# Attention keys stored by residue modulo 4, with the value rows and masks in that order

## The chip, the cores and the metric

The kernel runs on one core of one Trainium2 chip. The metric is device time in microseconds (us) of one execution. The core has five engines with queues of their own: TensorE (PE in the profile; its weight loads are listed as PEld), VectorE (DVE), ScalarE (ACT), GpSimd (POOL) and SyncE (SP), which here issues nearly all DMAs. Matrix products land in PSUM, eight banks of 2 KB per partition.

## The reference

One layer of a bidirectional encoder over 1024 positions of width 2048. A normalised input is multiplied by a large matrix; the columns feed 16 attention heads (64 wide), an HGRN2 recurrence, and gates; an output matrix, a residual, and a gated embedding follow. What matters here is the attention:

```python
DILATION_CFG = ((128, 1), (512, 4), (2048, 16))   # window, dilation

q = rope_partial(heads(aq, ATT_HEADS), pos) * (ATT_HD ** -0.5)
k = rope_partial(heads(ak, ATT_HEADS), pos)
v = heads(av, ATT_HEADS)
res = [dilated_band_attention(q, k, v, w, d) for (w, d) in DILATION_CFG]
outs = jnp.stack([r[0] for r in res])
lses = jnp.stack([r[1] for r in res])
alpha = jax.nn.softmax(lses, axis=0)
o_att = jnp.einsum('gbsh,gbshe->bshe', alpha, outs).reshape(B, S, ATT_W)
y_att = o_att * jax.nn.silu(ag.astype(f32))
```

A query attends to the positions at most 64 away (dilation 1), to those at most 256 away of the same residue modulo 4, and to those of the same residue modulo 16. The three are joined by their log denominators, which is one softmax over all of them, a key counting as often as it occurs.

## The kernel before

**Products in three parts.** Every large product is made of float32 data split in a high part (fp32r) and a low part (bf16): high times high, high times the weight's low part, low times the weight in bf16. A group of 128 output columns (`group_parts`, L95 to L110) takes four weight pieces of 512 rows. `piece` (L70 to L86) loads a piece on SP (`raw`), and makes `wh` on ScalarE (L83), `wl` on GpSimd (L84) and `wb` on VectorE (L85), each from a ring of three buffers. A piece is 24 matmuls of 512 columns, 12 for each half of the 1024 positions, and `group_parts` hands control back twice per piece, so that a group has eight parts. The sums stand in two of four PSUM banks called `gb`; the other four (`wk`) serve scores, transposes and outputs.

**Order.** A planner orders the instructions of each engine when the program is built, by their place in the program and by modelled durations, and each engine then runs its queue strictly in that order. Instructions marked with `high_priority` (the pieces) are drawn forward. Work that stands later in the program can be placed earlier where the planner thinks that an engine would wait.

**The attention stage** works on eight pairs of heads (`Pair`), two heads of 64 in 128 partitions.

- `keys` (L550 to L574) makes a group of 128 columns. For each half, `rope_evac` copies it to `araw` (ScalarE, L521), sends four small DMAs on SP to `apart` (L525, L526), multiplies on GpSimd (L528) and VectorE (L529), and the callback adds the two (L560). The sum is then split in three bf16 tiles `ak`: for each head a cast on ScalarE (L566), a DMA that puts a copy into the other 64 partitions (L568, L570), a subtraction on VectorE (L567), and at last a cast on VectorE (L572). Keys lie in order of position, 1024 a row.
- `queries` and `q_half` (L576 to L606) do the like for the queries, which are written by residue modulo 4 within each block of 128; the split is `aqt`.
- `scores` (L620 to L672) makes eight units per half: four dilated ones, one per residue, in which 128 queries meet 256 keys of that residue (`KS[s][:, h, i::4]`), and four local ones, in which 128 queries (reordered in `aql`, L633) meet 256 neighbouring keys from `wstart(i)`. A unit is six matmuls (L642): two heads, three products. VectorE adds the mask and takes the maximum (L647), ScalarE makes the exponential and its sum (L649). After every second unit one part of another group, the `fill`, is issued, so that TensorE has work. Small steps on VectorE (L657 to L670) then join the denominators.
- `values` (L674 to L718) scales the weights (L690, L692), transposes them on TensorE (L694), copies them out of PSUM (L697), and multiplies with the value rows: L710 dilated with `avc`, L707 local with `avn`.
- `loads` (L608 to L618) fetches `avc` by two DMAs and `avn` by three: eleven tiles of 128 positions, which the local windows share.
- `gate` (L720 to L731) is a group whose callback multiplies the output `ayt` (sigmoid on ScalarE, L727; VectorE, L728; GpSimd, L729).

The main loop (L806 to L827) sets how these follow: for pair n, `a.scores(0)` with parts of a's gate as fill, four parts of pair n+1's queries, `a.values(0)`, `a.scores(1)` with the other four as fill, then this:

```python
            run(bq)
            if b:
                if n:
                    run(g, 2)
                run(b.keys(), 9)
                b.q_half(0)
            a.values(1)
            run(g)
```

For pair 0 four gate parts come before its scores, so none are left at this point. Small tiles (`araw`, `apr`, `aq`, `sg`) share a ring of five (`h2`).

Of the kernel before, what the change touches and what calls it, by code (L numbers as in the profile page):

```python
# [12 lines left out]
F32 = mybir.dt.float32  # L13
# [4 lines left out]
ALU = mybir.AluOpType  # L18
# [27 lines left out]
class Kern:  # L46
# [367 lines left out]
    def att_consts(self, positions):  # L414
# [35 lines left out]
        V.tensor_scalar(d, d, NEG, -NEG, op0=ALU.mult, op1=ALU.add)  # L450
        V.scalar_tensor_tensor(m, m, -math.log(2.0), d, op0=ALU.mult, op1=ALU.add)
        e2 = self.h2("ae2").bitcast(I32)[:, :384]
        nc.gpsimd.iota(e2, pattern=[[1, 384]], base=-128, channel_multiplier=0)
        m = MK[:, 384:]
        V.tensor_scalar(m, e2, tf, None, op0=ALU.subtract)
        V.tensor_tensor(m, m, m, op=ALU.mult)
# [76 lines left out]
        self.tc.add_manual_dep(inst.ins, mark.ins.name, mybir.DependencyInfo(mybir.DependencyClass.NoSync, mybir.DependencyReason.DATA),  # L533
                               reason="issue order")

    starts = [0, 128] + [128 * j - 64 for j in range(1, 8)] + [768, 896]

    @staticmethod
    def wstart(i):
        return 0 if i == 0 else (768 if i == 7 else 128 * i - 64)  # L540
# [1 line left out]
    class Pair:  # L542
# [7 lines left out]
        def keys(self):  # L550
            K, nat = self.K, self.nat
            nc = K.nc
            V = nc.vector
            self.KS = [K.big.tile([128, 2, S], BF16, name=f"ak{i}", tag=t, bufs=n)
                       for i, (t, n) in enumerate((("X", 2), ("X", 2), ("O", 1)))]

            def sink(hf, p):
                def fin(a, b):
                    sl = slice(512 * hf, 512 * hf + 512)
                    V.tensor_tensor(a, a, b, op=ALU.add)  # L560
                    for s in range(3):
                        for h in range(2):
                            n, m = nat[h], nat[1 - h]
                            kd = self.KS[s][n, h, sl]
                            if s < 2:
                                nc.scalar.copy(kd, a[n])  # L566
                                V.tensor_tensor(a[n], a[n], kd, op=ALU.subtract)  # L567
                                nc.sync.dma_start(self.KS[s][m, h, sl], kd)  # L568
                                if s == 0:
                                    nc.sync.dma_start(self.KS[2][m, h, sl], kd)  # L570
                            else:
                                V.tensor_copy(kd, a[n])  # L572
                K.rope_evac(False, hf, p, fin)
            return K.group_parts(self.w_in, 1024 + 128 * self.hp, sink)  # L574

# [32 lines left out]
        def loads(self):  # L608
            K, vsrc = self.K, self.vsrc
            nc = K.nc  # L610
            self.vn = K.big.tile([128, 11, 128], F32, name="avn", tag="ht", bufs=1)
            self.vc = K.big.tile([128, 4, 2, 128], F32, name="avc", tag="hvt", bufs=1)
            for k in range(2):
                nc.sync.dma_start(self.vc[:, :, k], vsrc[512 * k:512 * k + 512, :].rearrange("(p r) e -> p r e", r=4))
            for i0, n in ((0, 2), (2, 7), (9, 2)):
                t0 = K.starts[i0]
                nc.sync.dma_start(self.vn[:, i0:i0 + n], vsrc[t0:t0 + 128 * n, :].rearrange("(c p) e -> p c e", p=128))
            self.yt = K.big.tile([128, S], F32, name="ayt", tag="gt", bufs=1)  # L618

        def scores(self, hf, fill):  # L620
            K, KS, QT = self.K, self.KS, self.QT
            nc = K.nc
            V = nc.vector
            sm = [K.big.tile([128, 2, 4, 256], F32, name=f"asm{h}", tag=("F2", "Q2")[h], bufs=1) for h in range(2)]
            own = K.sp.tile([128, 2, 2, 2, 4], F32, name="aown", bufs=1)
            oth = K.sp.tile([128, 2, 2, 2, 4], F32, name="aoth", bufs=1)
            for u, (loc, i) in enumerate(((0, 0), (0, 1), (1, 0), (0, 2), (1, 1), (0, 3), (1, 2), (1, 3))):
                w0 = K.wstart(4 * hf + i)
                sc = K.wk("asc")
                if loc:  # L630
                    ql = K.big.tile([128, 4, 4, 32], BF16, name="aql", tag="aql", bufs=3)
                    src = QT.rearrange("p h s (r i b) -> p (h s) r i b", i=4, r=4)[:, :, :, i]
                    (nc.gpsimd.tensor_copy if i % 2 else nc.scalar.copy)(ql, src)  # L633
                for h in range(2):
                    for s, sq in ((0, 0), (1, 0), (2, 1)):
                        if loc:
                            st = ql[:, 2 * h + sq].rearrange("p r b -> p (r b)")
                            mv = KS[s][:, h, w0:w0 + 256]
                        else:
                            st = QT[:, h, sq, 128 * i:128 * i + 128]  # L640
                            mv = KS[s][:, h, i::4]
                        nc.tensor.matmul(sc[:, 256 * h:256 * h + 256], st, mv, start=(h == 0 and s == 0),  # L642
                                         stop=(s == 2), skip_group_check=True)
                ms = 384 + (w0 - 128 * (4 * hf + i) + 128) if loc else 128 - 128 * hf
                for h in range(2):
                    d = sm[h][:, loc, i]
                    V.tensor_tensor_reduce(out=d, in0=sc[:, 256 * h:256 * h + 256], in1=K.MK[:, ms:ms + 256], scale=1.0,  # L647
                                           scalar=3.0e38, op0=ALU.add, op1=ALU.min, accum_out=own[:, 0, loc, h, i:i + 1])
                    nc.scalar.activation(d, d, AF.Exp, scale=-1.0, bias=own[:, 0, loc, h, i:i + 1],  # L649
                                         accum_out=own[:, 1, loc, h, i:i + 1])  # L650
                if u % 2:
                    next(fill, None)
            for x in range(4):
                for y in range(4):
                    o = oth[32 * x:32 * x + 32].rearrange("p s l h i -> p (s l h) i")[:, :, y]
                    w = own[32 * y:32 * y + 32].rearrange("p s l h i -> p (s l h) i")[:, :, x]
                    V.tensor_copy(o, w)  # L657
            m = K.sp.tile([128, 2, 2, 4], F32, name="afm", bufs=1)
            e = K.sp.tile([128, 2, 2, 2, 4], F32, name="afe", bufs=1)
            for l in range(2):  # L660
                V.tensor_tensor(m[:, l], own[:, 0, l], oth[:, 0, 1 - l], op=ALU.min)
                V.tensor_tensor(e[:, 1, l], m[:, l], oth[:, 0, 1 - l], op=ALU.subtract)
            V.tensor_tensor(e[:, 0], m, own[:, 0], op=ALU.subtract)
            nc.scalar.activation(e, e, AF.Exp)
            V.tensor_tensor(own[:, 1], own[:, 1], e[:, 0], op=ALU.mult)
            for l in range(2):
                V.tensor_tensor(e[:, 1, l], e[:, 1, l], oth[:, 1, 1 - l], op=ALU.mult)
            V.tensor_tensor(m, own[:, 1], e[:, 1], op=ALU.add)
            V.reciprocal(m, m)
            V.tensor_tensor(m, m, e[:, 0], op=ALU.mult)  # L670
            self.sm[hf] = sm
            self.fac[hf] = m  # L672

        def values(self, hf):  # L674
# [24 lines left out]
            def use(n):  # L699
                l, i = steps[n]  # L700
                P = pt[n // 2][:, n % 2]
                for c in range(2):
                    for h in range(2):
                        hs = slice(64 * h, 64 * h + 64)
                        if l:
                            t = K.starts.index(K.wstart(4 * hf + i) + 128 * c)
                            nc.tensor.matmul(o[hs, 128 * i:128 * i + 128], vn[:, t, hs], P[:, h, c],  # L707
                                             start=False, stop=(n == 7 and c == 1), skip_group_check=True)
                        else:
                            nc.tensor.matmul(ov[hs, :, i, :], vc[:, i, c, hs], P[:, h, c].rearrange("p (i b) -> p i b", i=4),  # L710
                                             start=(n == 0 and c == 0), stop=False, skip_group_check=True)
# [23 lines left out]
def tile_hybrid(ctx, tc, x, p, positions, w_in, w_out, g_pre, g_post, g_hg, lb_fwd, lb_bwd, w_pg, w_pp, g_ple, out):  # L735
# [54 lines left out]
    with tc.tile_pool(name="big", bufs=1) as big:  # L790
# [8 lines left out]
        def run(parts, n=8):  # L799
            for _ in range(n):  # L800
                next(parts, None)
# [5 lines left out]
        for n, a in enumerate(heads):  # L807
            b = heads[n + 1] if n < 7 else None
            a.loads()
            g = a.gate()  # L810
            if n == 0:
                run(g, 4)
            a.scores(0, g)
            bq = b.queries() if b else iter(())
            run(bq, 4)
            if n == 7:
                run(g, 2)
            a.q_half(1)
            a.values(0)
            a.scores(1, bq if b else islice(g, 2))  # L820
            run(bq)
            if b:
                if n:
                    run(g, 2)
                run(b.keys(), 9)
                b.q_half(0)
            a.values(1)  # L827
            run(g)
# [258 lines left out]
```

## Time and profile before

| | |
|---|---|
| Median of 3 runs | 2933.66 us (2931.59 to 2936.01) |
| Profiled execution | 2931.53 us, of which the profile's span is 2929.7 us |
| Granted TensorE clock | 0.99 of full speed |
| TensorE busy | 2793.9 us (95%) |
| VectorE, ScalarE, GpSimd busy | 1541.4, 1022.2, 1045.4 us |
| Attention stage | about 1260 to 2125 us of the span |
| DMA queues | 28% of 16 engines' time |

A busy time is a sum over an engine's instructions, with overlaps counted once. Matmuls are pipelined, so the length of one is more than its share of TensorE's time; the step from one start to the next is that share. A row of a group gives line, engine, operation, the tile written and the tile read, the count, then busy time and mean length of one, then the idle time just before and what ended it. In the order of time a row gives start, length, engine, line and count. A row of waits gives the total, the number and the longest wait.

### The profile page before, as it was taken

How to read it: one execution, taken by the hardware profiler on the slowest of the kernel's cores; microseconds unless marked ns; L12 is line 12 of the kernel's file. 1: busy time of each engine (PE TensorE's matmuls, PEld its weight loads, DVE VectorE, ACT ScalarE, POOL GpSimd, SP SyncE). 2: the span in 40 equal slices, each digit the busy share in tenths (PEclk: the TensorE clock that was granted, in tenths of full speed). 3: DMA queues.
4: the chain of work that ended last, by engine and by line, in shares of the span. 5: the costliest groups of instructions: out<-in, count | busy, mean ns of one | idle time of the engine just before them, and what ended most of it. 6: DMA issues, size and time to landing. Idle time of an engine off the chain costs nothing. (4 is left out here: it accounts for less than half of the span.)

```text
span 2929.7 us, 45661 instructions
## 1 busy us (share of the span) xinstructions
PE 2793.9 (95%) x17360; PEld 1906.6 (65%) x17360; DVE 1541.4 (53%) x3265; ACT 1022.2 (35%) x2094; POOL 1045.4 (36%) x801
## 2 busy tenths in 40 slices
PE   6999999999999999999999999999999899999997
PEld 4666666676676676676666666666666566566564
DVE  8601116846346446445655665655655635545555
ACT  5311112212122112125655555555633223333323
POOL 2422223413323313322232232223244554666555
PEclk9999999999999999999999999999999999999998
DMA  6412221111111111121221221222244543443453
GB/s 228 121 51 79 79 83 45 58 55 41 55 51 45 51 53 43 51 71 46 75 75 39 70 76 48 64 79 72 81 142 126 159 149 95 125 120 108 144 155 112
DMA packets 255708, 250.47 MB, mean 85 GB/s; under 512 B 21632, under 2 KB 179328, under 8 KB 254336
## 3 DMA queue, kind: packets, MB, share of 16 engines
q1 hardware_dynamic: 246320, 238.62, 27.9%
q10 hardware_dynamic: 9168, 8.93, 0.9%
q8 instruction: 136, 2.23, 0.3%
q14 instruction: 84, 0.69, 0.1%
HBM read 205.54 MB, written 29.36 MB: 80 GB/s over the span
## 5 line engine op out<-in xcount | busy, mean ns | idle before, releaser
L84 POOL TENSOR_TENSOR wl<-raw,wh 128x512 fp32r<-128x512 f32 x568 | 769.8, 1359 | 1589.9 <-ACT wh L83 1537.3
L85 DVE CAST wb<-raw 128x512 bf16<-128x512 f32 x584 | 406.3, 699 | 769.6 <-PE gb L107 276.5
L83 ACT CAST wh<-raw 128x512 fp32r<-128x512 f32 x584 | 358.3, 617 | 1198.7 <-PE gb L102 374.6
L102 PE MATMUL gb<-uh,wh 128*128 128x512 f32 x1792 | 742.8, 415 | 1.6 <-ACT araw L521 1.6
L103 PE MATMUL gb<-uh,wl 128*128 128x512 f32 x1792 | 709.4, 396 | 0.0
L107 PE MATMUL gb<-ul,wb 128*128 128x512 bf16 x1792 | 434.8, 381 | 0.2 <-issue 0.2
L102 PEld LDWEIGHTS gb<-uh,wh 128*128 128x128 f32 x1792 | 338.1, 189 | 88.8 <-ACT araw L521 2.4
L103 PEld LDWEIGHTS gb<-uh,wl 128*128 128x128 f32 x1792 | 338.0, 189 | 70.7
L107 PEld LDWEIGHTS <-wb 128*128 128x128 bf16 x1792 | 158.2, 98 | 209.9 <-issue 55.7
L869 PE MATMUL gb<-wh,yh 128*128 128x512 f32 x512 | 230.7, 451 | 5.4 <-DVE Y L901 2.9
L869 PE MATMUL gb<-wh,th 128*128 128x512 f32 x480 | 215.2, 448 | 0.0
L870 PE MATMUL gb<-wl,yh 128*128 128x512 f32 x512 | 203.3, 398 | 6.2 <-POOL wl L84 6.2
L870 PE MATMUL gb<-wl,th 128*128 128x512 f32 x480 | 190.0, 396 | 6.2 <-POOL wl L84 6.2
L647 DVE CUSTOM_DVE_ANT_0 asm<-asc,amask 128x256 f32<-128x256 f32 x256 | 95.8, 422 | 125.0 <-PE asc L642 124.1
L649 ACT ACTIVATE asm<-asm,aown 128x256 f32<-128x256 f32 x256 | 127.3, 498 | 58.1 <-DVE aown L647 57.9
L873 PE MATMUL gb<-wb,yl 128*128 128x512 bf16 x512 | 138.5, 383 | 0.0
L873 PE MATMUL gb<-wb,tl 128*128 128x512 bf16 x480 | 129.3, 383 | 0.0
L869 PEld LDWEIGHTS gb<-wh,yh 128*128 128x128 f32 x512 | 97.7, 191 | 36.3 <-DVE Y L901 3.8
L766 PE MATMUL gb<-wh,uh 128*128 128x512 f32 x256 | 116.3, 461 | 1.8 <-ACT wh L83 1.8
L642 PE MATMUL asc<-ak,aqt 128*128 128x256 bf16 x384 | 96.8, 405 | 20.9 <-DMA ak<-ak 16.4
L870 PEld LDWEIGHTS gb<-wl,yh 128*128 128x128 f32 x512 | 97.3, 190 | 27.4 <-POOL wl L84 8.7
L767 PE MATMUL gb<-wl,uh 128*128 128x512 f32 x256 | 102.2, 406 | 9.3 <-POOL wl L84 5.6
(286 smaller groups left out, 3847.1 us busy)
## 6 DMA issues: line engine op xcount, KB each, us to landing
raw<-in_w_in_dram SPq DMA_DIRECT2D x320, 256.0 KB
raw<-in_w_out_dram SPq DMA_DIRECT2D x128, 256.0 KB
raw<-in_w_pg_dram SPq DMA_DIRECT2D x128, 256.0 KB
xt<-in_x_dram SPq DMA_DIRECT2D x8, 1024.0 KB
vD<-vo SPq DMA_DIRECT2D x32, 256.0 KB
raw<-yD SPq DMA_DIRECT2D x32, 256.0 KB
xr<-in_x_dram SPq DMA_DIRECT2D x32, 256.0 KB
ak<-ak SPq DMA_DIRECT2D x96, 64.0 KB
```

Of the source, the lines that this page charges most:

```text
L83: nc.scalar.copy(wh, raw)
L84: (sub or nc.gpsimd).tensor_tensor(wl, raw, f32(wh), op=ALU.subtract)
L85: nc.vector.tensor_copy(wb, raw)
L102: nc.tensor.matmul(pb[hf], wh[:, k], self.uh[hf][:, kt], start=(kt == 0), stop=False)
L103: nc.tensor.matmul(pb[hf], wl[:, k], self.uh[hf][:, kt], start=False, stop=False)
L107: mm = nc.tensor.matmul(pb[hf], wb[:, k], self.ul[hf][:, kt], start=False, stop=(kt == KT - 1))
L649: nc.scalar.activation(d, d, AF.Exp, scale=-1.0, bias=own[:, 0, loc, h, i:i + 1], accum_out=own[:, 1, loc, h, i:i + 1])
L766: nc.tensor.matmul(pb[t], hi, wh, start=(k == 0), stop=False)
L767: nc.tensor.matmul(pb[t], hi, wl, start=False, stop=False)
L869: nc.tensor.matmul(pb[t], a, pc[0], start=first, stop=False)
L870: nc.tensor.matmul(pb[t], a, pc[1], start=False, stop=False)
L873: nc.tensor.matmul(pb[t], lo[:, k, 128 * t:128 * t + 128], pc[2], start=False, stop=last)
```

## The change

Keys are stored by residue: column 256 r + c of a row holds position 4 c + r. The sum of a half goes to a new tile `akn` in that order, and casts, subtractions and DMAs work on four runs of 128 columns. A dilated unit reads 256 columns in a row, a local unit four runs of 64. The local mask is built in the same order and read as four runs, and the scores of a local unit leave in residue order, so the value rows of each local window are fetched in that order: eight windows of 2 x 128 rows (`avn` has 16 tiles for 11), by eight DMAs into 64 partitions each for three into 128. In the main loop the two gate parts ahead of the next pair's keys are gone from there, and `run(g)` after `a.values(1)` issues all that is left, four parts for pairs 1 to 6.

```diff
-        nc.gpsimd.iota(e2, pattern=[[1, 384]], base=-128, channel_multiplier=0)
+        nc.gpsimd.iota(e2.rearrange("p (r c) -> p r c", r=4), pattern=[[1, 4], [4, 96]], base=-128, channel_multiplier=0)
...
-                    sl = slice(512 * hf, 512 * hf + 512)
-                    V.tensor_tensor(a, a, b, op=ALU.add)
+                    kn = K.h2("akn")
+                    V.tensor_tensor(kn.rearrange("p (r c) -> p c r", r=4), a.rearrange("p (c r) -> p c r", r=4),
+                                    b.rearrange("p (c r) -> p c r", r=4), op=ALU.add)
+                    a = kn
                     for s in range(3):
                         for h in range(2):
                             n, m = nat[h], nat[1 - h]
-                            kd = self.KS[s][n, h, sl]
+                            ks = self.KS[s][:, h].rearrange("p (r c) -> p r c", r=4)[:, :, 128 * hf:128 * hf + 128]
+                            kd = ks[n]
+                            an = a[n].rearrange("p (r c) -> p r c", r=4)
                             if s < 2:
-                                nc.scalar.copy(kd, a[n])
-                                V.tensor_tensor(a[n], a[n], kd, op=ALU.subtract)
-                                nc.sync.dma_start(self.KS[s][m, h, sl], kd)
+                                nc.scalar.copy(kd, an)
+                                V.tensor_tensor(an, an, kd, op=ALU.subtract)
+                                nc.sync.dma_start(ks[m], kd)
...
-            self.vn = K.big.tile([128, 11, 128], F32, name="avn", tag="ht", bufs=1)
+            self.vn = K.big.tile([128, 8, 2, 128], F32, name="avn", tag="ht", bufs=1)
...
-            for i0, n in ((0, 2), (2, 7), (9, 2)):
-                t0 = K.starts[i0]
-                nc.sync.dma_start(self.vn[:, i0:i0 + n], vsrc[t0:t0 + 128 * n, :].rearrange("(c p) e -> p c e", p=128))
+            row = vsrc.ap[0][0]
+            for i0, st, n in ((0, 7, 2), (1, 1, 6)):
+                t0 = K.wstart(i0)
+                step = (K.wstart(i0 + st) - t0) * row
+                for r in range(4):
+                    src = bass.AP(tensor=vsrc.tensor, offset=vsrc.offset + (t0 + r) * row, ap=[[4 * row, 64], [step, n], [1, 128]])
+                    nc.sync.dma_start(self.vn[64 * (r % 2):64 * (r % 2) + 64, i0:i0 + st * (n - 1) + 1:st, r // 2], src)
...
-                            mv = KS[s][:, h, w0:w0 + 256]
+                            mv = KS[s][:, h].rearrange("p (r c) -> p r c", r=4)[:, :, w0 // 4:w0 // 4 + 64]
                         else:
                             st = QT[:, h, sq, 128 * i:128 * i + 128]
-                            mv = KS[s][:, h, i::4]
+                            mv = KS[s][:, h, 256 * i:256 * i + 256]
...
-                    V.tensor_tensor_reduce(out=d, in0=sc[:, 256 * h:256 * h + 256], in1=K.MK[:, ms:ms + 256], scale=1.0,
+                    V.tensor_tensor_reduce(out=d.rearrange("p (r c) -> p r c", r=4),
+                                           in0=sc[:, 256 * h:256 * h + 256].rearrange("p (r c) -> p r c", r=4), in1=mk, scale=1.0,
...
-                            t = K.starts.index(K.wstart(4 * hf + i) + 128 * c)
-                            nc.tensor.matmul(o[hs, 128 * i:128 * i + 128], vn[:, t, hs], P[:, h, c],
+                            nc.tensor.matmul(o[hs, 128 * i:128 * i + 128], vn[:, 4 * hf + i, c, hs], P[:, h, c],
...
-                if n:
-                    run(g, 2)
                 run(b.keys(), 9)
                 b.q_half(0)
```

More of the change, by code (lines that the diff above doesn't have):

```diff
@@ L534, in after @@
                                reason="issue order")
-    starts = [0, 128] + [128 * j - 64 for j in range(1, 8)] + [768, 896]
     @staticmethod
@@ L563, in fin @@
                             n, m = nat[h], nat[1 - h]
-                            kd = self.KS[s][n, h, sl]
+                            ks = self.KS[s][:, h].rearrange("p (r c) -> p r c", r=4)[:, :, 128 * hf:128 * hf + 128]
+                            kd = ks[n]
+                            an = a[n].rearrange("p (r c) -> p r c", r=4)
                             if s < 2:
-                                nc.scalar.copy(kd, a[n])
-                                V.tensor_tensor(a[n], a[n], kd, op=ALU.subtract)
-                                nc.sync.dma_start(self.KS[s][m, h, sl], kd)
+                                nc.scalar.copy(kd, an)
+                                V.tensor_tensor(an, an, kd, op=ALU.subtract)
+                                nc.sync.dma_start(ks[m], kd)
                                 if s == 0:
-                                    nc.sync.dma_start(self.KS[2][m, h, sl], kd)
+                                    nc.sync.dma_start(self.KS[2][m, h].rearrange("p (r c) -> p r c", r=4)[:, :, 128 * hf:128 * hf + 128], kd)
                             else:
-                                V.tensor_copy(kd, a[n])
+                                V.tensor_copy(kd, an)
                 K.rope_evac(False, hf, p, fin)
@@ L637, in scores @@
                             st = ql[:, 2 * h + sq].rearrange("p r b -> p (r b)")
-                            mv = KS[s][:, h, w0:w0 + 256]
+                            mv = KS[s][:, h].rearrange("p (r c) -> p r c", r=4)[:, :, w0 // 4:w0 // 4 + 64]
                         else:
                             st = QT[:, h, sq, 128 * i:128 * i + 128]
-                            mv = KS[s][:, h, i::4]
+                            mv = KS[s][:, h, 256 * i:256 * i + 256]
                         nc.tensor.matmul(sc[:, 256 * h:256 * h + 256], st, mv, start=(h == 0 and s == 0),
                                          stop=(s == 2), skip_group_check=True)
-                ms = 384 + (w0 - 128 * (4 * hf + i) + 128) if loc else 128 - 128 * hf
+                if loc:
+                    ms = (w0 - 128 * (4 * hf + i)) // 4 + 32
+                    mk = K.MK[:, 384:].rearrange("p (r c) -> p r c", r=4)[:, :, ms:ms + 64]
+                else:
+                    mk = K.MK[:, 128 - 128 * hf:384 - 128 * hf].rearrange("p (r c) -> p r c", r=4)
                 for h in range(2):
                     d = sm[h][:, loc, i]
-                    V.tensor_tensor_reduce(out=d, in0=sc[:, 256 * h:256 * h + 256], in1=K.MK[:, ms:ms + 256], scale=1.0,
+                    V.tensor_tensor_reduce(out=d.rearrange("p (r c) -> p r c", r=4),
+                                           in0=sc[:, 256 * h:256 * h + 256].rearrange("p (r c) -> p r c", r=4), in1=mk, scale=1.0,
                                            scalar=3.0e38, op0=ALU.add, op1=ALU.min, accum_out=own[:, 0, loc, h, i:i + 1])
```

## The prediction

> **What bounds the kernel now.** I read the head of the page first, then the busy times by stage, then the waits of TensorE, and last the order of its instructions around the changed lines.
>
> ```profile
> span 2929.7 us, 45661 instructions
> PE 2793.9 (95%) x17360; PEld 1906.6 (65%) x17360; DVE 1541.4 (53%) x3265; ACT 1022.2 (35%) x2094; POOL 1045.4 (36%) x801
> ```
> ```profile
> core 0: us, PE busy (x) PEld busy (x) DVE busy (x) ACT busy (x) POOL busy (x), PEclk, DMA share, GB/s
> ...
> 1260.00:2125.00 865.00, 827.01 (x4763) 568.24 (x4762) 511.32 (x1543) 468.69 (x1112) 228.95 (x183) 0.99 0.24 67
> ```
> The attention stage lies at about 1260 to 2125 us. TensorE is busy in 827 of 865 us there, the next engine in 511. So a microsecond of TensorE work is a microsecond of the span, unless a wait opens in its place. The waits that exist:
>
> ```profile
> PE asc L642 <- DMA ak<-ak: 16.4, 6, 3.9
> ...
> PE asc L642 <- ACT sg L727: 4.5, 2, 2.4
> PE apt L694 <- DVE asm L692: 4.2, 3, 2.1
> ...
> PE gb L102 <- ACT araw L521: 1.6, 2, 1.0
> ```
> The first two rows are eight waits, one at the first scores of each pair, 20.9 us together: the split keys are not there yet. The last row is a group's PSUM bank that ScalarE has not emptied.
>
> But busy time can hide slow work. The scores have two kinds, both 128x256 in bf16: dilated ones (stationary aqt, every fourth key read) and local ones (stationary aql, 256 keys in a row).
>
> ```profile
> L642 PE MATMUL asc<-ak,aqt x384: 385/407/437, 1337.1 to 2088.8; 128*128 128x256 bf16 x192
> ...
> L642 PE MATMUL asc<-ak,aql x384: 270/273/421, 1337.5 to 2090.3; 128*128 128x256 bf16 x192
> ```
> Durations overlap, so I take starts (pair 3, order of time on TensorE; columns are start and length):
>
> ```profile
> 1675.73 0.82 PE L642 MATMUL asc<-ak,aql 128*128 128x256 bf16 x6
> 1676.38 1.53 PE L642 MATMUL asc<-ak,aqt 128*128 128x256 bf16 x6
> 1677.73 1.04 PE L107 MATMUL gb<-ul,wb 128*128 128x512 bf16 x4
> ```
> Six local matmuls hold TensorE for 1676.38 - 1675.73 = 0.65 us, six dilated ones for 1677.73 - 1676.38 = 1.35 us. Same shape, same type, same PSUM form; what differs is the step of 8 bytes between the moving keys.
>
> **Part 1: dilated keys become contiguous.** A unit (six matmuls) then should cost what a local one does: 0.65 for 1.35, a gain of 0.70 us. 384 matmuls are 64 units: 64 x 0.70 = 44.8 us off TensorE. Ends: 0 (the step isn't the cause) and 44.8; I take 44.8, because the local row is the contiguous case itself.
> By the Trainium skill (Advanced Engine Details and Errata, SBUF Cachelines) an access pattern keeps full speed when it hits each 16-byte line at least twice; a step of 8 bytes does that. By this rule the dilated read costs nothing extra and the gain is 0; the two rows above speak against it.
>
> **Part 2: local keys become four runs of 64.** No row has this read. Ends: 0.65 us a unit as now (a run is contiguous, only its start jumps, three jumps in 256 columns) and 1.35 (the stepped rate). I take 0.65, nearest to what a run is; the other end is a rival.
>
> **Part 3: the gate piece ahead of the next keys goes behind the values.** For pairs 1 to 6 two parts, one weight piece, move: a load on SP, a cast on ScalarE, a subtraction on GpSimd, a cast on VectorE and 24 matmuls (1621.04 to 1626.35 below: 5.3 to 5.4 us). Nothing is saved; the question is which waits move.
>
> First, the keys now start straight after the queries, and want the banks that the queries just filled. At pair 0 this already is so:
>
> ```profile
> 1392.78 0.58 PE L102 MATMUL gb<-uh,wh 128*128 128x512 f32 x1
> 1394.33 0.50 PE L102 MATMUL gb<-uh,wh 128*128 128x512 f32 x1 [0.96 <-ACT araw L521]
> ```
> ScalarE's evacuation stands behind the exponentials and scalings of the scores. Six pairs more at 0.96 us: +5.8 us. Ends: 0 (a later evacuation is covered by the other half) and twice that, +11.6.
>
> Second, the 10.8 us of gate work behind the values should cover the late keys. I think it does not, for a reason in the order. Transition to pair 3 first, then to pair 1:
>
> ```profile
> 1621.04 0.50 PE L102 MATMUL gb<-uh,wh 128*128 128x512 f32 x1
> ...
> 1626.35 0.58 PE L102 MATMUL gb<-uh,wh 128*128 128x512 f32 x1
> ...
> 1631.74 0.58 PE L102 MATMUL gb<-uh,wh 128*128 128x512 f32 x1
> 1634.26 0.61 PE L642 MATMUL asc<-ak,aqt 128*128 128x256 bf16 x2 [1.94 <-DMA ak<-ak]
> ```
> ```profile
> 1419.38 0.50 PE L102 MATMUL gb<-uh,wh 128*128 128x512 f32 x1
> ...
> 1430.08 0.58 PE L102 MATMUL gb<-uh,wh 128*128 128x512 f32 x1
> 1433.52 0.61 PE L642 MATMUL asc<-ak,aqt 128*128 128x256 bf16 x2 [2.86 <-DMA ak<-ak]
> ```
> In both, exactly two pieces and one matmul stand between the values and the scores, though the program leaves one piece at pair 2's end and none at pair 0's. The planner fills the place with the next pair's own gate work until it thinks the keys are ready, and the keys are 2 to 3 us later than it thinks. After the change the two pieces are the old gate's, and the wait stays. What is gained is order: pair n+1 keeps its two pieces for between its scores.
>
> **Part 4: the keys' own chain.** The final sum writes with a step of 512 bytes; the queries' sum, which does so already, is the row for it:
>
> ```profile
> L582 DVE TENSOR_TENSOR aq<-araw,apr 128x512 f32<-128x512 f32 x13 | 14.0, 1078 | 13.8 <-POOL apr L528 13.8
> ...
> L560 DVE TENSOR_TENSOR araw<-araw,apr 128x512 f32<-128x512 f32 x14 | 9.7, 692 | 5.7 <-POOL apr L528 4.7
> ```
> 1078 - 692 = 0.39 us. Casts and subtractions keep counts and contiguous rows of 128. The new buffer akn makes three tiles a half in a ring of five; the second half then waits for the first half's sum, which it does in the order of now anyhow: no cost, at worst one GpSimd product of 1.3 us.
>
> The 96 half-moving DMAs have 256 packets of 256 bytes for 64 of 1 KB. Two stretches, one with the keys' moves and one with the queries' (512-byte packets):
>
> ```profile
> q1 hardware_dynamic: 420, 0.34, 30.6%
> ```
> ```profile
> q1 hardware_dynamic: 1056, 0.51, 29.8%
> ```
> ```profile
> L568 SPq DMA_DIRECT2D ak<-ak x64: 472/546/557, 1322.0 to 2045.3; - x64
> ```
> ```profile
> L617 SPq DMA_DIRECT2D avn<-vD x24: 366/461/1452, 1260.4 to 2047.8; - x24
> ```
> Per packet 0.306 x 4.5 us x 16 / 420 = 52 ns and 0.298 x 7.3 us x 16 / 1056 = 33 ns (the stretches are 1621.3 to 1625.8 and 1652.7 to 1660.0 us). A small packet costs between 0 and 33 ns: at most 256 x 33 / 16 = 0.53 us a DMA for 64 x 52 / 16 = 0.21. SP issues one per 0.55 us and stays the limit, so only the last one counts, +0.3.
>
> V takes eight DMAs for three, 1024 KB for 704: five more issues at 0.46 = 2.3 us on SP. They stand near the second half's key moves:
>
> ```profile
> 1628.05 0.97 SPq L617 DMA_DIRECT2D avn<-vD  x2
> 1630.69 0.51 SPq L568 DMA_DIRECT2D ak<-ak  x1
> ```
> SP was free from 1629.02 to 1630.69 = 1.7 us; 0.6 is left. Behind a late key move are its partner's cast and the first scores, so TensorE waits that long. Together +0.39 + 0.3 + 0.6 = 1.3 us at seven transitions: +9.
>
> Against that, the gate's evacuation leaves the chain for pairs 2 to 7:
>
> ```profile
> 1621.33 1.40 DVE L567 TENSOR_TENSOR araw<-araw,ak 64x512 f32<-64x512 f32 x2 [0.68 <-ACT ak L566]
> ...
> 1629.93 0.69 DVE L728 TENSOR_TENSOR sg<-gb,sg 128x512 f32<-128x512 f32 x1
> 1630.70 4.75 DVE L567 TENSOR_TENSOR araw<-araw,ak 64x512 f32<-64x512 f32 x4
> ```
> The evacuation takes 0.69 us, and four subtractions took 4.75 where the first half's took 1.40 for two, 2.0 us more: relief between 0 and 2.7, taken as 1.3, at six: -8. Net +1; ends -14 (all waits of these six gone; they sum 14.1) and +10.
>
> **Part 5: what faster scores expose.** Pairs 0 and 1 have no fill left between their scores, which run in a clump. The factors' chain on VectorE already ends last at pair 1's values (1.4 of the 4.2 us row above). Four dilated units are 2.8 us shorter there, so each pair gives back between 0 and 2.8; I take half, +3. Elsewhere fill is there:
>
> ```profile
> L649 ACT ACTIVATE asm<-asm,aown 128x256 f32<-128x256 f32 x224 | 111.4, 498 | 52.6 <-DVE aown L647 52.5
> ...
> L647 DVE CUSTOM_DVE_ANT_0 asm<-asc,amask 128x256 f32<-128x256 f32 x224 | 84.0, 422 | 115.9 <-PE asc L642 115.1
> ```
> By busy time over count, eight units cost VectorE 16 x 0.375 = 6.0 us and ScalarE 16 x 0.50 = 8.0, beside two pieces and eight units on TensorE, 10.8 + 5.2.
>
> Rows of mask and masked sum in four runs, the iota, and V's matmuls (same shapes) I cost at nothing: VectorE is idle a third of the stage. Were each masked sum slower as the key sum is (x 1.56), 9.4 us would still fit in 16.
>
> **The sum.** -44.8 + 5.8 + 1 + 3 = -35. The profiled execution took 2931.5 us (span 2929.7); 2931.5 - 35 = 2896.5. It lay 2.1 under the median of 2933.7, so the median to expect is 2898.6, say 2899.
>
> **The rivals.**
> *The cover works*: the planner leaves the scores behind two whole pieces and the chain is quicker than the evacuations made it, so the six waits go. For it: the waits are only 2 to 3 us. Against: pair 1, where the fill was whole and the wait longest. Time: 2899 - 15 = 2884.
> *Local runs pay* (slower): if 64-wide runs are read at the stepped rate, 64 local units lose 0.70 each, the dilated gain is cancelled, and +5.8 + 1 + 3 stay: 2931.5 + 10 + 2.1 = 2943. It decides from 0.65 + 35/64 = 1.20 us a local unit. Against: only three jumps per matmul.
> *The step isn't the cause* (the change doesn't do what it says): dilated units stay at 1.35; also 2943. The two rows leave little else: PSUM and stationary are alike. This is the page's cacheline rule as a rival.
> *The key moves choke*: were small packets to go through half as fast as SP issues, six in a row would end 6 x 0.55 = 3.3 us later, at seven pairs +23: 2922. The Trainium skill (DMA: Bandwidth & Descriptors, Specifications) asks for 512 bytes for full line rate, which speaks for this; no row has a 256-byte packet.
>
> **How the numbers follow.** Forecast 0.70, the cover works 0.10, choked moves 0.08, local runs 0.07, step not the cause 0.05. Its own range is 2884 (the waits of part 4 gone) to 2916 (the upper ends of parts 3, 4 and 5 at once, +5.8 + 9 + 2.6). For 8 in 10 I go from 2879 to 2921. Less than 0.2% (5.9 us) can't be told from no change. Faster takes the first three, less a share of the choked case: 0.87; slower 0.08, same 0.05.
>
> **What would show it.** Six dilated matmuls at 0.65 us, six local ones unchanged (Parts 1 and 2: either at 1.35 breaks the forecast). The row of TensorE waiting for araw at about eight times in place of two (Part 3). Two pieces and one matmul still ahead of each pair's scores, with waits of 2 to 4 us on the keys (Part 3 and 4). A wait of TensorE for VectorE's scaling at pairs 0 and 1 over 1.4 us (Part 5). The forecast is wrong if the wait for the keys passes 6 us a pair, or if a new wait opens in the fills.

## The result, and the profile after

The changed kernel takes 2917.19 us (median of 5 runs, 2914.93 to 2921.35) where the kernel before takes 2933.66: a ratio of 0.9944, 95% interval 0.993 to 0.9959. The gain is 16.5 us. The forecast was 2899 us, a gain of 35. So the sign holds, and the time lies within the 2879 to 2921 us that were given for 8 in 10; it is 1 us above the forecast's own range, 2884 to 2916, and less than half of the forecast gain arrived. The profiled execution took 2914.93 us.

The head of the page after, and the row of the whole attention stage, from the end of the recurrence to the end of the last values (start and end, length, then busy time of each engine, TensorE's granted clock, DMA share and rate):

```profile
span 2912.8 us, 45468 instructions
...
PE 2745.8 (94%) x17117; PEld 1898.4 (65%) x17360; DVE 1553.8 (53%) x3265; ACT 1019.0 (35%) x2094; POOL 1036.4 (36%) x801
```
```profile
core 0: us, PE busy (x) PEld busy (x) DVE busy (x) ACT busy (x) POOL busy (x), PEclk, DMA share, GB/s
1290.50:2098.60 808.10, 749.71 (x4503) 532.92 (x4561) 513.88 (x1514) 456.48 (x1096) 210.21 (x175) 0.98 0.26 70
```
The same stage of the kernel before:

```profile
1290.30:2115.10 824.80, 786.81 (x4563) 539.68 (x4561) 498.06 (x1514) 458.84 (x1096) 217.96 (x175) 0.99 0.24 65
```
The stage is 824.8 - 808.1 = 16.7 us shorter, which is the whole gain. TensorE is busy 37 us less, but idle 808.1 - 749.7 = 58.4 us where it was 824.8 - 786.8 = 38.0. A further loss stands in the clock. I took the granted clock in stretches of 2 us and summed what is missing to full speed: 8.5 us before, 15.3 after. Work at full clock is then 824.8 - 38.0 - 8.5 = 778.3 before and 808.1 - 58.4 - 15.3 = 734.4 after, a difference of 43.9. That is a little too much: some 60 records of matmuls are missing from the stage after, and their time looks idle. TensorE's waits in the stage sum to 54.7 us (eight rows, seven of them below and 2.9 for `aPT` from VectorE), where those of before sum to 37.9; so 3.7 of the 58.4 us are probably missing records. By the waits, some 40 us of work are gone (44.8 forecast); 16.8 us came back as waits and 6.8 as a slower clock.

First the scores, in groups by shape (count, then busy time and mean ns, then idle time just before), before and after:

```profile
L642 PE MATMUL asc<-ak,aqt 128*128 128x256 bf16 x384 | 96.8, 405 | 20.9 <-DMA ak<-ak 16.4 <-ACT sg L727 4.5
L642 PE MATMUL asc<-ak,aql 128*128 128x256 bf16 x384 | 51.4, 278 | 0.0
```
```profile
L648 PE MATMUL asc<-ak,aql 128*128 128x256 bf16 x384 | 52.6, 282 | 5.8 <-DVE aown L657 5.8
L648 PE MATMUL asc<-ak,aqt 128*128 128x256 bf16 x384 | 51.9, 275 | 14.0 <-DMA ak<-ak 14.0
```
The dilated group falls from 96.8 to 51.9 us, the local one stays. In the order of time on TensorE (start, length):

```profile
1672.08 0.82 PE L648 MATMUL asc<-ak,aql 128*128 128x256 bf16 x6
1672.74 0.82 PE L648 MATMUL asc<-ak,aqt 128*128 128x256 bf16 x6
1673.39 1.03 PE L107 MATMUL gb<-ul,wb 128*128 128x512 bf16 x4
```
Six local matmuls, now in four runs of 64, take 0.66 us from start to start, six dilated ones 0.65.

Where the idle time grew, in TensorE's waits after (total, times, longest):

```profile
PE asc L648 <- DMA ak<-ak: 14.0, 8, 3.2
...
PE apt L705 <- DVE asm L703: 8.9, 5, 2.7
PE ao L717 <- ACT aPT L708: 8.6, 5, 2.0
...
PE gb L102 <- ACT araw L521: 6.7, 7, 1.0
PE asc L648 <- DVE aown L657: 5.8, 5, 1.8
...
PE gb L877 <- DVE sg L738: 4.3, 2, 2.4
PE gb L102 <- DVE sg L738: 3.5, 1, 3.5
```
Before, the keys were waited for 20.9 us in all, `araw` 1.6 and the scaled weights (`asm`) 4.2. Now the keys are 14.0, and every other row shown is larger or new. The row of `aown` is a bank that the masked sums still hold: the scores run into VectorE. No single wait has taken the place of the gain; it went in pieces of 1 to 3 us.

### The profile page after: what moved, and what is told of

The parts are those of the page before. It is cut to its first block, busy times and chain, and to the rows that moved or that the text cites. A ratio compares the mean times of both kernels' runs of the same rounds, so it can differ in the third digit from the quotient of the medians.

```text
span 2912.8 us, 45468 instructions
## 1 busy us (share of the span) xinstructions
PE 2745.8 (94%) x17117; PEld 1898.4 (65%) x17360; DVE 1553.8 (53%) x3265; ACT 1019.0 (35%) x2094; POOL 1036.4 (36%) x801
## 5 line engine op out<-in xcount | busy, mean ns | idle before, releaser
L85 DVE CAST wb<-raw 128x512 bf16<-128x512 f32 x584 | 427.0, 734 | 757.8 <-PE gb L107 252.8
L107 PE MATMUL gb<-ul,wb 128*128 128x512 bf16 x1643 | 407.9, 380 | 8.9 <-issue 1.4
L877 PEld LDWEIGHTS gb<-wh,th 128*128 128x128 f32 x480 | 90.8, 189 | 27.2 <-ACT sg L981 2.0
L878 PEld LDWEIGHTS gb<-wl,th 128*128 128x128 f32 x480 | 90.4, 188 | 26.3 <-POOL wl L84 8.9
```

The costliest lines, as they stand in the source:

```text
L85: nc.vector.tensor_copy(wb, raw)
L107: mm = nc.tensor.matmul(pb[hf], wb[:, k], self.ul[hf][:, kt], start=False, stop=(kt == KT - 1))
L877: nc.tensor.matmul(pb[t], a, pc[0], start=first, stop=False)
L878: nc.tensor.matmul(pb[t], a, pc[1], start=False, stop=False)
```

## The experiments

Two questions stood at the start: does the step of 8 bytes alone explain the dilated scores, and which part of the change gives the time back?

**The step alone.** In the kernel before, dilated units read 256 keys in a row (the wrong keys; all else stays):

```diff
-                            mv = KS[s][:, h, i::4]
+                            mv = KS[s][:, h, 256 * i:256 * i + 256]
```


> The kernel before, but each dilated score matmul reads 256 neighbouring key columns instead of every fourth one (so it meets the wrong keys; no other instruction differs). Theory A, the prediction's part 1 with part 5: six dilated matmuls take 0.65 us, 44.8 us of TensorE work go, about 3 come back at pairs 0 and 1, time 2933.7 - 42 = 2892. Theory B: the rate is right, but VectorE and ScalarE now end last in the scores and in the joining of the denominators, and about a third of the gain comes back as waits at every pair: 2933.7 - 28 = 2906. If the step were not the cause: 2934.

Measured: 2899.61 us, ratio 0.9883 (0.987 to 0.9897), a gain of 33.4. The scores become equal (groups by shape first, then the stage's row):

```profile
L642 PE MATMUL asc<-ak,aqt 128*128 128x256 bf16 x384 | 55.3, 278 | 24.6 <-DMA ak<-ak 21.2 <-ACT wh L83 1.9 <-DVE ak L572 1.5
L642 PE MATMUL asc<-ak,aql 128*128 128x256 bf16 x384 | 51.4, 277 | 0.0
```
```profile
1290.00:2082.00 792.00, 744.98 (x4563) 529.68 (x4562) 496.41 (x1514) 457.40 (x1097) 216.85 (x175) 0.99 0.25 68
```
The step is the cause of the slow reads. No record is missing here (4563 matmuls as before), and with 6.8 us of clock loss the work gone is 778.3 - (745.0 - 6.8) = 40.1 us, less than the 44.8 forecast. Of the forecast gain a quarter does not arrive even here, where nothing else was changed: idle time is 792.0 - 745.0 = 47.0 us for 38.0. So faster scores expose 9 us of waits by themselves, most of them at the values, where TensorE waits 14.9 us for the copies `aPT` that took 8.1 before; a wait for `aown` does not occur. The other 18 us that the change loses against this kernel come from its other parts.

**The new buffer alone.** In the kernel before, the sum goes to `akn`, in the old order of keys:

```diff
-                    V.tensor_tensor(a, a, b, op=ALU.add)
+                    kn = K.h2("akn")
+                    V.tensor_tensor(kn, a, b, op=ALU.add)
+                    a = kn
```


> The kernel before, but the keys' final sum goes to a fresh tile akn of the ring of five, in the old order of columns (no strided write, old DMAs, old reads). Theory A, the ring: three tiles a half leave no place for the second half's copy until the first half's sum is done, its four small DMAs then stand behind the first half's key moves on SP, and the keys come some 7 us later at each of seven transitions; the planner covers part of it, 5 to 15 us slower: 2939 to 2949. Theory B, the prediction's part 4 (no cost, at worst one GpSimd product of 1.3 us a pair): 2934, at most 2940.

Measured: 2929.67 us, ratio 0.9988 (0.9979 to 0.9997): nothing, if anything a gain of 3.4. The loss that I expected did not come. The profile has the attention stage 2.0 us longer than before; what is gained lies behind it, where the kernel takes 808.8 us for 814.6.

**The gate's move alone.** In the kernel before, the two gate parts ahead of the keys go behind the values:

```diff
-                if n:
-                    run(g, 2)
```


> The kernel before without the two gate parts ahead of the next keys (they follow the values, as in the changed kernel). Theory A, the prediction's part 3: six waits of 0.96 us for the evacuation of araw come, two pieces and one matmul still stand ahead of the scores, the waits for the keys stay or lose up to 1.3 us each: 2933.7 + 5.8 - 8 to + 5.8, so 2931 to 2940. Theory B, the cover works: the six waits go, 2933.7 + 5.8 - 14 = 2925.

Measured: 2940.07 us, ratio 1.0023 (1.0011 to 1.0035), 7.0 slower. Its waits:

```profile
PE asc L642 <- DMA ak<-ak: 22.3, 8, 4.2
PE gb L102 <- ACT araw L521: 7.9, 7, 2.1
```
The `araw` row goes from 2 times to 7 and from 1.6 to 7.9 us, and the keys are waited for as before. The moved parts cover nothing.

**The buffer taken out of the changed kernel, two ways.** First, GpSimd writes its product in residue order and the sum goes into that tile, so that `akn` is not needed:

```diff
+            nc.gpsimd.tensor_tensor(pr.rearrange("p (r c) -> p c r", r=4), pt.rearrange("p (c r) -> p c r", r=4),
+                                    self.RS[:, sl].rearrange("p (c r) -> p c r", r=4), op=ALU.mult)
...
-                    kn = K.h2("akn")
-                    V.tensor_tensor(kn.rearrange("p (r c) -> p c r", r=4), a.rearrange("p (c r) -> p c r", r=4),
-                                    b.rearrange("p (c r) -> p c r", r=4), op=ALU.add)
-                    a = kn
+                    V.tensor_tensor(b.rearrange("p (r c) -> p r c", r=4), a.rearrange("p (c r) -> p r c", r=4),
+                                    b.rearrange("p (r c) -> p r c", r=4), op=ALU.add)
+                    a = b
```


> The changed kernel without the tile akn: GpSimd writes its product in residue order, and the sum is made in place of it. Theory A, the ring: the second half's small DMAs are again ahead of the first half's key moves, the keys' chain loses about 7 us a pair, waits of TensorE for VectorE's masked sums and for PSUM banks at the start of the scores go: 5 to 15 us faster than the changed kernel, 2902 to 2912. Theory B: the ring costs nothing, GpSimd's strided write (one more unknown) adds up to 1 us a half to the chain: 2917 to 2922.

Second, `akn` stays but gets a buffer outside the ring of five; to make room the two score masks share one tile and one mask of the recurrence lies on another, so scores and recurrence get wrong masks:

```diff
-                    kn = K.h2("akn")
+                    kn = K.big.tile([128, 512], F32, name="akn", tag="akn", bufs=1)
```


> The changed kernel with a place of its own for akn (one tile outside the ring of five). To make room the local mask lies on the dilated one and one HGRN selection mask on another, so scores and recurrence get wrong masks; every instruction stays with its shape. Theory A, the ring is what cost the changed kernel 19 us against the in-place sum: 2895 to 2905. Theory B, the gain of the in-place sum came from elsewhere (the product made in residue order, or another order by chance): 2912 to 2920.

Measured: 2898.11 us (ratio 0.987, 0.9857 to 0.9884) and 2897.42 us (0.988, 0.9866 to 0.9894), both 19 faster than the change, the first by more than expected. So it is not the extra write, nor the order in which it is written, but the place in the ring. DMA issues on SP show what the ring does. The kernel before first, then the changed one, around pair 3's keys (start, length; `apart` are the rotation's small moves, `ak` the key moves):

```profile
1619.83 0.62 SPq L525 DMA_DIRECT2D apart<-araw  x1
1621.33 0.53 SPq L568 DMA_DIRECT2D ak<-ak  x1
...
1625.10 0.68 SPq L526 DMA_DIRECT2D apart<-araw  x1
```
```profile
1612.65 0.67 SPq L570 DMA_DIRECT2D ak<-ak  x1
...
1615.42 1.27 SPq L570 DMA_DIRECT2D ak<-ak  x2
1616.74 0.70 SPq L525 DMA_DIRECT2D apart<-araw  x1
1618.96 0.37 SPq L76 DMA_DIRECT2D raw<-in_w_in_dram  x1
1619.38 0.69 SPq L526 DMA_DIRECT2D apart<-araw  x1
1620.12 0.64 SPq L525 DMA_DIRECT2D apart<-araw  x1
1620.81 0.62 SPq L526 DMA_DIRECT2D apart<-araw  x1
...
1627.06 0.62 SPq L570 DMA_DIRECT2D ak<-ak  x1
```
And with the sum in place (`e4`):

```profile
1603.85 0.62 SPq L525 DMA_DIRECT2D apart<-araw  x1
1604.52 0.62 SPq L526 DMA_DIRECT2D apart<-araw  x1
1605.19 0.62 SPq L525 DMA_DIRECT2D apart<-araw  x1
1607.13 0.67 SPq L573 DMA_DIRECT2D ak<-ak  x1
...
1611.31 0.70 SPq L526 DMA_DIRECT2D apart<-araw  x1
...
1617.23 0.61 SPq L573 DMA_DIRECT2D ak<-ak  x1
```
In place, three of the second half's four `apart` moves go out ahead of the first half's key moves, as in the kernel before. With `akn` all four stand behind the six key moves. It is so at all seven transitions. From the first half's first key move to the last `apart`: 1611.31 - 1607.13 = 4.2 us in place, 1620.81 - 1612.65 = 8.2 us with the ring. The second half's keys are later by that, and from the last key matmul to the first scores of pair 3 it is 29.2 us after the change, 23.4 in place and 21.8 before.

**The gate parts put back into the changed kernel**, alone and together with the sum in place:

```diff
+                if n:
+                    run(g, 2)
```


> The changed kernel with the two gate parts ahead of the next keys again. Theory A, the move costs what it cost the kernel before (7 us, by six waits for araw): 2917 - 7 = 2910. Theory B, the extra gate work behind the values hides part of the longer key chain of the changed kernel, and without it more of the next pair's fill is drawn forward and the scores run in a clump: 2917 to 2925.

> The changed kernel with the in-place sum and with the two gate parts ahead of the next keys again. Theory A, the move costs 7 us here too: 2898 - 7 = 2891. Theory B, the extra gate work behind the values is worth its six waits: 2898 to 2905.

Measured: 2905.06 us (ratio 0.9905, 0.9892 to 0.9917), 12 faster than the change and below both expectations; and 2899.25 us (0.9888, 0.9875 to 0.9901). The second is the kernel with only the order left of the change: sum, moves, masked sums and value loads by residue. It equals the first experiment's 2899.61, which has none of these. So the new order with all its copies costs nothing that can be measured. And the gate's move costs nothing once the ring is relieved (2898.11 for 2899.25), but 12 us beside it. The ring costs 5.8 us with the gate parts in their old place (2905.06 for 2899.25) and 19 with them moved; both together cost 17.9. Not all of the 12 us lie in the attention stage: the profiles end its values at 2093.6 and 2098.6 us, 5.0 apart, and behind them take 807.0 and 814.2 us. Why the rest is quicker there, as with the buffer alone, no run tells.

**The value loads alone**: two DMAs of 128 partitions in place of eight of 64, in the changed kernel (other rows than wanted are fetched):

```diff
-            for i0, st, n in ((0, 7, 2), (1, 1, 6)):
...
+            for i0 in (0, 8):
+                nc.sync.dma_start(vf[:, i0:i0 + 8], vsrc.rearrange("(c p) e -> p c e", p=128))
```


> The changed kernel, but V's local rows come by two DMAs into 128 partitions in place of eight into 64, the same 1024 KB, in the old order of rows (so the local values are the wrong rows). Theory A, the prediction's 0.6 us a transition: 2917 - 4 = 2913. Theory B, six issues fewer on SP at about 0.6 us, which stand ahead of the second half's key moves, shorten the key chain by up to 3.6 us a pair, of which half shows: 2917 - 12 = 2905.

Measured: 2916.46 us (ratio 0.9949, 0.9936 to 0.9961), 0.7 under the change. Six issues fewer, and nothing moves.

**Ring and gate's move together, without faster scores.** Each alone cost -3.4 and +7.0. Is it the pair, or do they need the faster scores? Both edits above in the kernel before:

> The kernel before with both costs and none of the gain: the sum in a fresh tile akn of the ring, old order of columns, and the gate parts moved behind the values. Alone they gave -3 and +7 us. Theory A, the two multiply each other whatever the speed of the scores (12 us more together, as in the changed kernel, where each alone costs about 6 or nothing): 2931.5 - 3 + 7 + 12 = 2948. Theory B, the extra cost needs the fast dilated units, which run away from VectorE while it still splits the late keys: 2931.5 - 3 + 7 = 2935.

Measured: 2954.73 us, ratio 1.0072 (1.006 to 1.0085), 21.9 slower. The pair does it: 18.3 us more than the sum of the two, with dilated reads as slow as ever. In the stage alone the buffer costs 2.0 us, the move 7.3 and both 24.8, so there the pair adds 15.5. The account comes near: -33.4 for the faster scores and +21.9 for ring and move make -11.5, 5 us from the measured -16.5. Its waits:

```profile
PE asc L644 <- DMA ak<-ak: 14.8, 9, 3.0
PE gb L102 <- ACT araw L521: 8.8, 7, 2.0
```
The buffer alone has the same order on SP and is covered; there the gate's two parts stand between the queries and the keys. Why the cover fails with the parts gone is seen only as more waits of several kinds: the stage's idle time is 50.8 us, where it is 37.5 and 42.3 with one edit, and its clock loss 17.1, where it is 10.2 in both. It is not that the keys come later still: from the last key matmul to the first scores it is 24.6 to 25.9 us with the buffer alone and 23.4 to 25.4 with both. Which of these waits starts the others, no run here tells. The gate's own tile `sg` comes from the same ring, so the move also shifts its place there; no run separates that from the lost cover.

**A step further.** In the changed kernel with the sum in place, ScalarE's waits remain (8.3 us for `aPT`). Its copies that reorder the queries (`aql`) can go to GpSimd, which does half of them already; I tried that without and with the gate parts put back:

```diff
-                    (nc.gpsimd.tensor_copy if i % 2 else nc.scalar.copy)(ql, src)
+                    nc.gpsimd.tensor_copy(ql, src)
```


> The changed kernel with the in-place sum, and all 64 reorderings of the queries (aql) on GpSimd, where half were on ScalarE. Theory A, what is left of the lost gain is ScalarE's and VectorE's lag behind TensorE at the values (8 us of waits for ScalarE's aPT, 7 for VectorE's scaling): ScalarE loses 20 us of work and some 5 to 8 us of the waits go, 2890 to 2893. Theory B, GpSimd's copies come later than ScalarE's did, or the waits hang on VectorE alone: 2897 to 2903.

> As the run before, with the gate parts ahead of the next keys. Theory A: 2899 - 5 to 8 = 2891 to 2894. Theory B: 2899 to 2904.

Measured: 2888.34 us, ratio 0.9851 (0.9838 to 0.9865), against 2903.8 us, 0.9902 (0.9887 to 0.9917). The first is 44.5 under the kernel before and 28.9 under the change, the fastest kernel here. Its largest waits:

```profile
PE asc L651 <- DMA ak<-ak: 12.4, 7, 5.9
PE apt L708 <- DVE asm L706: 7.2, 5, 2.2
PE gb L102 <- ACT araw L521: 6.7, 7, 1.0
```
The wait for ScalarE's `aPT` is gone. In the second the same edit leaves it 4.6 us above the kernel without it, with intervals that overlap; no gain at least:

```profile
PE asc L651 <- DMA ak<-ak: 13.3, 7, 4.0
PE ao L723 <- DVE aPT L711: 11.0, 8, 2.0
PE asc L651 <- DVE aown L660: 9.6, 7, 2.1
```
Two waits for VectorE sum to 20.6 us, where the same kernel with half of the copies on ScalarE has 15.1. So the gate's move gains 15 us where GpSimd makes these copies, nothing without that (1.1), and costs 7 in the kernel before and 12 beside the ring. The order of the rest decides what it is worth.

## Why the prediction was right or wrong, by its steps

**Part 1 (dilated keys contiguous, -44.8): right.** Six matmuls take 0.65 us, and the work gone from the stage is about 40 us; where the other 4 us of the 64 units stay, no run tells. By the Trainium skill (SBUF — State Buffer, the paragraph on SBUF "cachelines"), a bf16 pattern may step up to 8 elements at no loss; a step of 4 here cost 0.70 us per six matmuls, so the measurement decides against it for this operand. The rival that rested on that rule falls.

**Part 2 (local runs at nothing): right.** 51.4 us busy before, 52.6 after. The rival that these pay falls.

**Part 3, the `araw` term (+5.8): the waits right in kind and size, their price only for the kernel before.** 7 waits of 0.96 us came; alone, the move cost 7.0 us, and the cover did not work. With the ring relieved the same seven waits come and the move costs nothing: against them, waits for the keys fall from 15.5 to 10.2 us and those for `aown` from 5.3 to 1.0. So there the moved parts do cover, which the forecast denied. The figure of "two pieces and one matmul" ahead of each pair's scores was wrong: at pair 3 there are three pieces and a part of a fourth.

```profile
1629.40 0.40 PE L103 MATMUL gb<-uh,wl 128*128 128x512 f32 x1
1632.17 0.44 PE L648 MATMUL asc<-ak,aqt 128*128 128x256 bf16 x2 [2.37 <-DMA ak<-ak]
1632.40 1.49 PE L648 MATMUL asc<-ak,aql 128*128 128x256 bf16 x6
```
The run of this fill began at 1611.97, right after the values, and 17.4 us later the keys were still not there. The wait at the scores (14.0 us in all) therefore did not grow with the delay. I take it that the fill used up here was missing later; no run shows that by itself.

**Part 4 (the key chain, +1): the step that failed, and in it the sentence on `akn`, "no cost".** The forecast looked at what the second half waits for among the engines' sums and not at the order of SP's queue: with a third tile from the ring, the second half's four `apart` moves went behind the first half's six key moves. Without the ring place the same kernel is 19 us faster. The cost depends on Part 3's move: without it, the buffer costs nothing in the kernel before and 5.8 us in the changed one. So a sum of terms, each priced by itself, could not have shown it; the two were 18 us more than their sum. As far as is known this step failed because the ring changed SP's order; how the late keys and the moved gate parts together come to so much stays open. The rest of Part 4 holds: the strided sum takes 1.08 us as its row promised, the 256-byte moves and V's eight DMAs cost nothing (2899.25 for 2899.61; 0.7 us). The rival of choked moves named a time near the measured one (2922) by another mechanism, and falls: the moves were late, not slow. By the Trainium skill (DMA: Bandwidth & Descriptors, Specifications) moves under 512 bytes fall short of line rate. The traces show no shortfall that counts: a packet of the key moves took 18 ns (median) for 256 bytes and 67 for 1 KB before, 14 and 15 bytes per ns. A move is then 256 x 18 / 16 = 0.29 us on 16 engines, less than SP's issue of one, 0.59 us where it took 0.55.

**Part 5 (what faster scores expose, +3): too small, and elsewhere than thought.** At pairs 0 and 1 the waits for the scaled weights are 2.7 and 2.4 us, where pair 1 had 1.4. But with faster reads alone they are absent there; the changed kernel without ring place and move has them (2.2 and 1.9 us), so they come with the new order of the keys. And "elsewhere fill is there" was wrong: with faster reads alone the stage has 9 us more idle, and the change shows five waits for `aown`, 5.8 us.

The sum by measured terms: -40 of work, +23.6 of waits and clock. The forecast had -44.8 and +10. With the ring relieved the changed kernel takes 2898.11 us, within 1 us of the forecast; that is luck in part, as its stage has 41.3 us less work and 7.3 more of idle time and clock.

## What to carry to other kernels

A tile taken from a shared ring is an edit to the order of every queue that its users feed; read the order of the DMA queue around it before costing it at nothing, or write into a tile that is dying anyway. Two edits that each cost little can cost much together, so run them together and singly before keeping both. A gain in work on the bounding engine is worth its full size only where what feeds that engine has slack: here faster reads alone took some 40 us of work off TensorE and returned 33.4.

## What the runs showed of the hardware that was not expected

A wait of 2.3 us on TensorE can cost nearly as much again in clock. After the 2.37 us wait for pair 3's keys (TensorE alone; granted clock, DMA share and rate behind its count):

```profile
core 0: us, PE busy (x), PEclk, DMA share, GB/s
1630.00:1632.00 2.00, 0.00 (x0) 1.00 0.24 52
1632.00:1634.00 2.00, 1.83 (x10) 0.60 0.60 166
1634.00:1636.00 2.00, 2.00 (x8) 0.55 0.61 194
1636.00:1638.00 2.00, 2.00 (x13) 1.00 0.41 142
```
```profile
1634.33 0.63 PE L103 MATMUL gb<-uh,wl 128*128 128x512 f32 x1
1634.76 0.63 PE L102 MATMUL gb<-uh,wh 128*128 128x512 f32 x1
...
1636.61 0.39 PE L103 MATMUL gb<-uh,wl 128*128 128x512 f32 x1
```
Matmuls start 0.43 us apart for 3.4 us, then 0.23: 2 x 0.40 + 2 x 0.45 = 1.7 us lost. In the stage this happens 5 times before, 7 times after (once for 10.2 us) and 10 times with ring and gate's move in the kernel before, which makes the clock's share of 8.5, 15.3 and 17.1 us. The seven waits of 0.96 us show none. The clock's record shows which waits do: it comes in stretches of 3.41 us with their borders on one fixed grid. Between 1290 and 2130 us of the 13 profiles, every stretch at full clock in which TensorE was idle for more than 2.0 us was followed by one at half clock (54 of 54), of those with 1.7 to 2.0 us idle 21 of 44, of those with less 6 of 3009 (ends of matmuls are modelled, so idle time is known to some tenths of a us). So what tells is the idle time within one stretch, not the length of a wait: in the kernel before, a wait of 3.08 us that ends at 1737.4 us is cut by a border at 1736.3 in 1.99 and 1.08 us and shows no loss. By the Trainium skill (TensorE: Matmul & The Clock Gate, What's actually happening) the clock halves after an idle window of about 3.4 us that runs freely; the traces agree with the window, but 2 us of idle time within one were enough.

And one more tile of 2 KB per partition in a ring of five, which no engine's busy time shows, moved the changed kernel by 19 us.
